# Attention: low products of two key tiles in the two halves of the array, values stored by head, fetches spread, and the order ranked by a table

## The chip, the cores and the metric

The kernel runs on one core of a Trainium2 chip. Its time is the device time of one execution in microseconds (us); the span is the time from the first to the last instruction of the profiled execution. The core has five engines, each with an instruction queue of its own that it works through in order: PE (TensorE, products and transposes by identity), DVE (VectorE), ACT (ScalarE), POOL (GpSimd) and SP (SyncE, which here issues DMAs). PE's weight loads are a row of their own, PEld, and run beside its products. Data lies in SBUF in 128 partitions, and PE writes into 8 banks of PSUM of 128 partitions x 512 f32 each.

## The reference

A two-layer decoder trunk over 2048 tokens of width 1024: a Mamba-2 layer, then multi-head latent attention with 16 heads, whose keys and values come from the stream after the first layer. The change lies in the causal attention:

```python
for i in range(S // Q_BLOCK):
    ...
    s = jnp.einsum('bqhd,bkhd->bhqk', q_nope[:, q0:kv_len], k_nope[:, :kv_len]) + \
        jnp.einsum('bqhr,bkr->bhqk', q_rope[:, q0:kv_len], k_rope[:, :kv_len])
    s = s.astype(jnp.float32) * scale
    p = jax.nn.softmax(jnp.where(mask, s, -jnp.inf), axis=-1).astype(v.dtype)
    outs.append(jnp.einsum('bhqk,bkhd->bqhd', p, v[:, :kv_len]))
```

The head's key has 64 + 32 (rotated) channels, its value 64. Everything is f32 in the reference.

## The kernel before

**Pairs of f16.** To keep f32 accuracy with fast products, a number is split into a high and a low f16 half. A score is three products (`mm3`, lines L291, L292, L293: high x high, high x low, low x high). A head's values lie in SBUF as 128 keys x 128 columns, 64 high and 64 low, so that one product of a probability tile with all 128 columns gives both; the two halves of the result's rows are added at the end.

**Stages.** Until about 2057 us the Mamba layer, the projections and the latent keys and values run; their results go to DRAM (`kn_d`, `kr_d` for keys without and with rotation, `qn_d`, `q1_d`, `q2_d` for queries, `v_d` for values). From 2057 to 2823 us attention runs, then the output projection (`back`), whose first steps a scheduler places among the last ones of attention. All but attention is ordered by that scheduler.

**Attention** is 64 jobs n: 16 heads x 4 query blocks of 512 (qb 0 to 3), each with 4·qb + 4 key tiles k of 128. A group c is four key tiles (512 keys), and j counts the four query tiles of a block. Tiles on the diagonal are narrower: 512, 384, 256 and 128 queries. A job's tasks have letters, and the profile shows them by these lines:

- S (L291 to L293, and L1453 for the mask): the scores of query tile j and group c into a bank, on PE. M (L1466) the row maximum and N (L1471, L1472) the shift, on DVE; E (L1477) the exponential into an f32 tile `Pr`, on ACT.
- Then a tile of probabilities has to be turned (keys on the partitions). Two ways: for the groups in TURNED (c = 0 in qb 1, c = 0 and 1 in qb 2 and 3), L (L1482, L1483, POOL) splits it into high and low f16 in `HL`, and X (L1487) turns it by a transposing DMA from SP's queue into `PX`, eight tiles of 128 x 512, four high and four low. For the others, T (L1491) turns it on PE into a bank, A (L1496, ACT) copies the high half and B (L1500, DVE) the low half into `PTs`.
- V (L1511, L1512): two products for each key tile, with the high and with the low probabilities, summed in one bank. F (L1516, ACT) and C (L1520, DVE) add the bank's two halves, and O (L1538) stores them.
- D (L1388, L1389, L1395, L1401 to L1403): fetches of the next head's K, V and Q on SP's queue. At the first score of each qb the Q of that block is fetched (three DMAs), and at qb 2 also K (two DMAs) and V (one), ahead of it.

**What sets the order.** `Pace` plays the tasks through with fixed durations and waiting times and writes down in which order they start; that is the order of every engine in the program. It tries eight plans of what PE prefers, and takes the shortest by its own account. Value products go in a fixed order: the tiles turned on PE first, those turned by DMA last. Buffers: 16 `Pr`, 5 `PTs`, 6 `HL`, 3 `PX`, 8 banks.

In the middle of the kernel, `L1099` (Mamba) and `L975` write products of 64 rows into a bank:

```python
for t in (slice(0, 64), slice(64, P)):
    nc.tensor.matmul(yi[t, hc], E[:, h, t], Xd[:, hc], start=True, stop=True)   # L1099
...
nc.tensor.matmul(ps[0:2 * H, :], w[:, k].rearrange("p n h -> p (n h)"), xT[k][:, n, :],   # L975, H = 32
...
nc.tensor.transpose(ps[:, c * 2 * H:(c + 1) * 2 * H], rt[:, c * P:(c + 1) * P],  # L982
                    self.ident[0:2 * H, 0:2 * H])
```

Of the kernel before, what the change touches and what calls it, by code (L numbers as in the profile page):

```python
# [22 lines left out]
P = 128  # L23
# [5 lines left out]
NH = 16  # L29
# [12 lines left out]
ENGINES = ("PE", "ACT", "DVE", "POOL", "SP")  # L42
# [3 lines left out]
TURNED = ((), (0,), (0, 1), (0, 1))  # L46

# [23 lines left out]
class Pace:  # L71

    def __init__(self, turned, prefer, scored, reserve):

        self.turned, self.now, self.count = turned, 0.0, 0
        self.prefer, self.most, self.reserve = prefer, scored, reserve
        self.jobs = [(h, qb) for h in range(NH) for qb in range(NB)]
        self.todo_s, self.todo_t, self.todo_v = [], [], []
        for n, (h, qb) in enumerate(self.jobs):
            self.todo_s += [(n, j, c) for j in range(4) for c in range(qb + 1)]  # L80
            tiles = [(n, k) for k in range(4 * qb + 4)]
            here = [t for t in tiles if t[1] // 4 not in turned[qb]]
            self.todo_t += here
            self.todo_v += here + [t for t in tiles if t not in here]
        for todo in (self.todo_s, self.todo_t, self.todo_v):
            todo.reverse()
        self.spare = {k: deque(range(n)) for k, n in BUFS.items()}
        self.slot = {}
        self.scored, self.sums = 0, []
        self.until = {e: 0.0 for e in ENGINES}  # L90
        self.ready = {e: [] for e in ENGINES if e != "PE"}
        self.coming, self.order = [], []
        self.maxima, self.probs, self.pairs, self.opened, self.dma = {}, {}, {}, {}, {}

# [7 lines left out]
    def at(self, t, f):  # L102
        self.count += 1
        heapq.heappush(self.coming, (t, self.count, f))

    def issue(self, e, what, busy, delay=0.0, after=None):
        self.order.append(what)
        self.until[e] = self.now + busy
        self.at(self.until[e], lambda: None)
        if after:  # L110
            self.at(self.until[e] + delay, after)

    def queue(self, e, rank, start, fits=lambda: True):
        self.count += 1
        self.ready[e].append((rank, self.count, fits, start))
# [7 lines left out]
    def run(self):  # L123
        while True:
            for e, waiting in self.ready.items():
                if self.until[e] <= self.now:
                    fit = sorted((w for w in waiting if w[2]()), key=lambda w: w[:2])
                    if fit:
                        waiting.remove(fit[0])
                        fit[0][3]()  # L130
            if self.until["PE"] <= self.now:
                self.tensor()
            if not self.coming:
                break
            self.now = self.coming[0][0]
            while self.coming and self.coming[0][0] <= self.now:
                heapq.heappop(self.coming)[2]()
        assert not (self.todo_s or self.todo_t or self.todo_v)
        return self.order

    def tensor(self):
        banks = len(self.spare["ps"])
        if self.sums and banks:
            return self.rows(self.sums.pop())
        for kind in self.prefer:
            if kind == "S" and self.todo_s and banks > self.reserve and self.scored < self.most:
                return self.scores(*self.todo_s.pop())
            if kind == "T" and self.todo_t and banks and self.spare["PTs"]:
                n, k = self.todo_t[-1]
                if all((n, j, k // 4) in self.probs for j in range(self.first(n, k), 4)):  # L150
                    return self.turn(*self.todo_t.pop())
            if kind == "V" and self.todo_v and self.todo_v[-1] in self.pairs:
                if banks or self.todo_v[-1][0] in self.opened:
                    return self.values(*self.todo_v.pop())

    def scores(self, n, j, c):
# [3 lines left out]
        if j == c == 0:  # L160
            self.queue("SP", 2, lambda: self.issue("SP", ("D", n), 3500 if qb == 2 else 1800))

        def maximum():
            self.issue("DVE", ("M", n, j, c), 65 + w * 1.042, 116, counted)

        def counted():
            self.maxima[n, j] = self.maxima.get((n, j), 0) + 1
            if self.maxima[n, j] == qb + 1:
                self.queue("DVE", 1, lambda: self.issue("DVE", ("N", n, j), 250 if qb else 70, 120, shift))

        def shift():
            for x in range(qb + 1):
                self.queue("ACT", 2, lambda x=x: self.exp(n, j, x), lambda: self.spare["Pr"])

        self.issue("PE", ("S", n, j, c), 3 * (w / 2.4 + 2.5) + 60 * (c == qb), 200,
                   lambda: self.queue("DVE", 2, maximum))

    def exp(self, n, j, c):
        w = self.width(n, j, c)
        self.take("Pr", n, j, c)  # L180

        def freed():
            self.give("ps", "S", n, j, c)
            self.scored -= 1

        def done():
            if (j, c) == (3, NB - 1):
                self.queue("DVE", 3, lambda: self.issue("DVE", ("R", n), 450, 2000, summed))
            if c in self.turned[self.jobs[n][1]]:
                self.queue("POOL", 1, lambda: self.split(n, j, c),  # L190
                           lambda: self.spare["HL"] and ((n, c) in self.dma or self.spare["PX"]))
            else:
                self.probs[n, j, c] = w // P

        def summed():
            self.sums.append(n)

        self.issue("ACT", ("E", n, j, c), 245 + w * 0.832, 175, freed)
        self.at(self.until["ACT"] + 330, done)

    def split(self, n, j, c):
# [5 lines left out]
        def moved():  # L207
            self.give("Pr", n, j, c)
            self.queue("SP", 1, lambda: self.issue("SP", ("X", n, j, c), 1550, DMA_DELAY, landed))

        def landed():
            self.give("HL", n, j, c)
            self.dma[n, c] -= 1
            if not self.dma[n, c]:
                for k in range(4 * c, 4 * c + 4):
                    self.pairs[n, k] = "PX"
# [3 lines left out]
    def rows(self, n):  # L220
        self.take("ps", "Y", n)
        self.issue("PE", ("Y", n), 110, 200, lambda: self.queue("ACT", 2, lambda: self.issue(
            "ACT", ("Z", n), 160, 200, lambda: self.give("ps", "Y", n))))

    def turn(self, n, k):
        jj = self.first(n, k)
        w = (4 - jj) * P
        self.take("ps", "T", n, k)
        self.take("PTs", n, k)

        def done():
# [4 lines left out]
            self.queue("ACT", 1, lambda: self.issue("ACT", ("A", n, k), 55 + w * 0.835, 150,  # L236
                                                    lambda: self.queue("DVE", 1, low)))

        def low():
            self.issue("DVE", ("B", n, k), 65 + w * 1.042, 260, split)  # L240

        def split():
            self.give("ps", "T", n, k)
            self.pairs[n, k] = "PTs"
# [3 lines left out]
    def values(self, n, k):  # L248
        w, qb = (4 - self.first(n, k)) * P, self.jobs[n][1]
        if n not in self.opened:  # L250
            self.opened[n] = 4 * qb + 4
            self.take("ps", "O", n)
        self.opened[n] -= 1
        last = not self.opened[n]

        def done():
            if self.pairs[n, k] == "PTs":
                self.give("PTs", n, k)
            else:
                c = k // 4  # L260
                self.dma[n, c] -= 1
                if self.dma[n, c] == -4:
                    self.give("PX", n, c)
            if last:
                self.queue("ACT", 0, lambda: self.issue("ACT", ("F", n), 620, 60, lambda: self.queue(
                    "DVE", 0, lambda: self.issue("DVE", ("C", n), 598, 260, closed))))

        def closed():
            self.give("ps", "O", n)
            self.queue("SP", 0, lambda: self.issue("SP", ("O", n), 600))  # L270

        self.issue("PE", ("V", n, k), 2 * (w / 2.4 + 2.5), 200, done)


class Net:
# [987 lines left out]
    def mla_kv_down(self, b, tables):  # L1263
# [13 lines left out]
        self.rope(pk[0], pk[1], *tables, self.kr_d[0:16], self.kr_d[16:32], 16, b * TB,  # L1277
# [31 lines left out]
    def mla_up(self, b, tables):  # L1309
# [31 lines left out]
        while ahead:  # L1341
            (n, w), ahead = ahead, next(todo, None)
            qT = self.qT
            for i in range(2 if n == 6 else 4):
# [4 lines left out]
                elif n < 4:  # L1349
# [7 lines left out]
                    c0 = (n - 2) * 1024  # L1357
# [385 lines left out]
```

## Time and profile before

| | us |
|---|---|
| median of 3 runs (3016.37 to 3019.53) | 3016.63 |
| profiled execution, its own time | 3009.45 |
| its span | 3007.7 |
| PE busy in the span | 2892.3 (96%) |
| DVE busy | 2160.8 (72%) |
| ACT busy | 1813.6 (60%) |
| POOL busy | 977.0 (32%) |
| attention, first score to last value product | 2057 to 2823 |

A row of a group or timeline reads: line, engine, operation, written tile <- read tiles, shape (for PE "rows*columns" of the weights used, then the moving data), count; busy time and mean ns; and behind a bar or in brackets the idle time before it with what ended it. A product's busy time covers its drain too, which lies under the next one; so in a stream the distance of the starts is its price. "mm" and "tr" are the two names of the banks. SPq rows are the instructions of SP's queue, which issue DMAs.

### The profile page before, as it was taken

Reading aid. Unit: us, or ns where it says so; the run is one execution under the profiler, and the core shown is the slowest. Engines: PE = TensorE matmul, PEld = TensorE weight load, DVE = VectorE, ACT = ScalarE, POOL = GpSimd, SP = SyncE. Lnnn points to the kernel's source line nnn. Section 1 sums busy time; section 2 is a strip of 40 time slices with the busy share of each in tenths; the row PEclk is TensorE's granted clock in tenths of the full one; section 3 lists DMA queues with packets and bytes.
Section 4 is the critical chain, followed back from the end, with each engine's and each line's share of the span. In section 5 each row is a group of like instructions: output and inputs, shape, how many; then the busy total and the mean of one; then the engine's idle time right before and its main releaser. Section 6 shows DMA issues by size and latency. Waiting matters only on the chain.

```text
span 3007.7 us, 48921 instructions
## 1 busy us (share of the span) xinstructions
PE 2892.3 (96%) x16535; PEld 1793.7 (60%) x16535; DVE 2160.8 (72%) x4539; ACT 1813.6 (60%) x4632; POOL 977.0 (32%) x1206
## 2 busy tenths in 40 slices
PE   8999999999999999999999999999999999998998
PEld 6777745555565555655566545544555555554687
DVE  6878887778777777878665564456887888877476
ACT  7888586566755546556553443335777777776422
POOL 1212021112121221212111121225777777777300
PEclk9999999999999999999999999999999999999999
DMA  5353657655565335554445655656899899999784
GB/s 184 102 162 96 212 179 264 192 163 171 192 222 180 125 113 188 191 190 168 140 140 205 233 176 175 201 178 154 170 169 176 166 175 172 171 182 193 178 273 160
DMA packets 586415, 532.21 MB, mean 177 GB/s; under 512 B 396770, under 2 KB 450274, under 8 KB 584724
## 3 DMA queue, kind: packets, MB, share of 16 engines
q1 hardware_dynamic: 574180, 490.94, 60.3%
q0 software_dynamic: 11984, 38.15, 3.4%
q8 instruction: 130, 2.13, 0.3%
q14 instruction: 121, 0.99, 0.1%
HBM read 332.21 MB, written 112.86 MB: 148 GB/s over the span
## 4 chain that ended last, share of the span: by engine, by line
PE 57%; DVE 14%; DMA 10%; ACT 9%; issue 5%; POOL 4%; SPq 1%; ACTq 0%; DVEq 0%; POOLq 0%
PE mm L291 11%; PE mm L293 11%; PE mm L292 11%; PE tr L291 4%; PE tr L293 4%; PE tr L292 4%; DVE cacc L895 3%; DMA PX<-HL 3%; DMA big<-cumT 1%; DMA wraw<-in_ssm_w_in_dram 1%; PE mm L1511 1%; ACT Xw L1092 1%; PE tr L1099 1%; PE mm L1512 1%; POOL HL L1482 1%
## 5 line engine op out<-in xcount | busy, mean ns | idle before, releaser
L1483 POOL TENSOR_TENSOR HL<-Pr,HL 128x512 f16<-128x512 f32 x320 | 369.8, 1156 | 25.5
L291 PE MATMUL mm<-xT,wsp 128*128 128x512 f16 (+1 forms) x800 | 308.7, 386 | 0.4 <-ACT wsp L329 0.4
L292 PE MATMUL mm<-xT,wsp 128*128 128x512 f16 (+1 forms) x800 | 306.0, 382 | 0.0
L293 PE MATMUL mm<-xT,wsp 128*128 128x512 f16 (+1 forms) x800 | 304.6, 383 | 0.4 <-DVE wsp L322 0.2
L1048 POOL TENSOR_TENSOR Xp<-Xw,Xp 128x512 fp32r<-128x512 f32 x64 | 86.5, 1351 | 610.4 <-ACT Xp L1047 597.9
L1482 POOL CAST HL<-Pr 128x512 f16<-128x512 f32 x320 | 195.7, 612 | 157.7 <-ACT Pr L1477 105.4
L1477 ACT ACTIVATE Pr<-mm,nm 128x512 f32<-128x512 f32 (+3 forms) x322 | 201.0, 629 | 71.0 <-DVE nm L1472 66.3
L1477 ACT ACTIVATE Pr<-tr,nm 128x512 f32<-128x512 f32 (+3 forms) x318 | 197.5, 626 | 66.4 <-DVE nm L1472 63.2
L291 PE MATMUL mm<-wsp,xT 128*128 128x512 f16 (+2 forms) x640 | 233.8, 367 | 3.5 <-ACT craw L889 2.2
L895 DVE SCALAR_TENSOR_TENSOR cacc<-craw,pack,cacc 128x512 f32<-128x512 f32 x288 | 217.3, 774 | 26.0 <-ACT cacc L893 24.2
L292 PE MATMUL mm<-wsp,xT 128*128 128x512 f16 (+2 forms) x640 | 233.3, 365 | 1.4 <-DVE wsp L330 1.3
L293 PE MATMUL mm<-wsp,xT 128*128 128x512 f16 (+2 forms) x640 | 232.8, 364 | 0.0
L1466 DVE TENSOR_REDUCE mx<-tr 128x1 f32<-128x512 f32 (+3 forms) x318 | 186.4, 604 | 45.5 <-PE tr L1453 30.9
L1466 DVE TENSOR_REDUCE mx<-mm 128x1 f32<-128x512 f32 (+3 forms) x322 | 190.8, 605 | 29.4 <-PE mm L293 14.9
L291 PE MATMUL mm<-wsp,yT 128*128 128x512 f32 x512 | 210.0, 411 | 1.5 <-DVE sz L925 1.1
L292 PE MATMUL mm<-wsp,yT 128*128 128x512 f32 x512 | 204.0, 399 | 0.0
L293 PE MATMUL mm<-wsp,yT 128*128 128x512 f32 x512 | 203.3, 398 | 0.0
L293 PEld LDWEIGHTS <-xT 128*128 128x128 f16 (+1 forms) x1280 | 125.0, 98 | 118.8 <-issue 4.9
L1076 ACT ACTIVATE big<-big,d_cum 128x128 f32<-128x128 f32 x512 | 168.1, 391 | 43.4 <-DMA big<-cumT 43.3
L292 PEld LDWEIGHTS <-xT 128*128 128x128 f16 (+1 forms) x1280 | 126.0, 98 | 114.4 <-issue 14.5
L291 PEld LDWEIGHTS <-xT 128*128 128x128 f16 (+1 forms) x1280 | 125.6, 98 | 115.1 <-issue 6.8
L1092 ACT ACTIVATE Xw<-tr,d_wend 128x64 f32<-128x64 f32 x512 | 111.7, 328 | 129.4 <-DVE y L1089 102.8
(469 smaller groups left out, 7735.8 us busy)
## 6 DMA issues: line engine op xcount, KB each, us to landing
wsp<-wo_d SPq DMA_DIRECT2D x96, 512.0 KB, 3.8
wsp<-w_d SPq DMA_DIRECT2D x68, 512.0 KB, 4.2
wraw<-in_ssm_w_in_dram SPq DMA_DIRECT2D x128, 256.0 KB, 3.2
big<-cumT SPq DMA_DIRECT2D x64, 512.0 KB, 4.9
wo_d<-wsp SPq DMA_DIRECT2D x32, 512.0 KB, 3.5
w_d<-wsp SPq DMA_DIRECT2D x32, 512.0 KB, 3.5
st<-w_d SPq DMA_DIRECT2D x56, 256.0 KB, 2.9
wsp<-wu_d SPq DMA_DIRECT2D x28, 512.0 KB, 3.7
```

The costliest lines, as they stand in the source:

```text
L291: mm(out, l_hi, r_hi, start=start, stop=False)
L292: mm(out, l_hi, r_lo, start=False, stop=False)
L293: mm(out, l_lo, r_hi, start=False, stop=stop)
L895: nc.vector.scalar_tensor_tensor(acc, raw[:, k:k + TB], wk[k], acc, ALU.mult, ALU.add)
L1048: nc.gpsimd.tensor_tensor(u[:, 1], x, u[:, 0].bitcast(F32), ALU.subtract)
L1076: act(E[:, h, :], E[:, h, :], AF.Relu, bias=ncum[:, h0 + h:h0 + h + 1])
L1092: act(Xw[:, hc], px[:, hc], AF.Copy, scale=wend[:, h0 + h:h0 + h + 1])
L1099: nc.tensor.matmul(yi[t, hc], E[:, h, t], Xd[:, hc], start=True, stop=True)
L1466: v.tensor_reduce(m[:, at:at + 1], s, AX.X, ALU.max, negate=True)
L1477: nc.scalar.activation(tile("Pr", n, j, c)[:, :w], bank("S", n, j, c)[:, :w], AF.Exp, bias=moves[(4 * n + j) % len(moves)], accum_out=sums ...
L1482: nc.gpsimd.tensor_copy(u[:, 0], x)
L1483: nc.gpsimd.tensor_tensor(u[:, 1], x, u[:, 0], ALU.subtract)
```

## The change

The high and low product of a key tile are separated. For the tiles in LOWS (4 tiles in qb 1, all 12 in qb 2, all 16 in qb 3), V does the high product only; when a block's tiles have had theirs, a new task W multiplies the low probabilities with the high values alone, 64 columns wide: even tiles into partitions 0 to 63 of the bank, odd ones into 64 to 127, in turn. (The product of low values and low probabilities is left out there.) High and low tiles have buffers of their own for this, `PH` (5) and `PL` (14, eight of them in the unused half of a key buffer, four in a former activation tile).

Values are stored by head (`v_d` is 16 x 128 x 16 x 128), so that a head's are read in one piece of 4 KB per partition. Rotated queries and keys are stored with both halves of the rotation side by side, and the rotated keys, which are the same for all heads, stay in both key buffers instead of being fetched for every head. The next head's Q comes in two fetches of two DMAs (at qb 0 and 2), K in two halves (qb 1 and 2), V at qb 3. Q, K and V have fixed places by head.

The order is no longer the best of eight plans. Each task has a rank from a table (by letter and place in the head) plus its head's number, and each engine starts the ready task of the lowest rank. Value products may go in any order within a block, and two blocks may be open at once.

```diff
-BUFS = dict(ps=8, Pr=16, PTs=5, HL=6, PX=3)
-PLANS = [(p, s, r) for p in ("TSV", "STV") for s in (5, 6) for r in (0, 1)]
+BUFS = dict(ps=8, Pr=16, PH=5, PL=14, HL=6, PX=3)
+MOST = 6
+DRAIN = 212
+LOWS = ((), ((0, 1, 2, 3),), (tuple(range(12)),), (tuple(range(16)),))
+RANKS = {
+    "S": "7735 344 732 4486 -631 9611 -3703 222 -978 281 305 -101 4274 -1728 204 3590 -1046 173 8785 "
...
+    def key(self, task):
+        kind, n, *at = task
+        h, qb = self.jobs[n]
...
+        return h + self.rank[kind][i] - 100 * (kind in "CFZ")
...
+    def do_V(self, n, k):
...
+        both = not self.paired(n, k)
...
+        self.issue("PE", ("V", n, k), (1 + both) * (w / 2.4 + 2.5), 200, done)
+
+    def do_W(self, n, g):
+        group = LOWS[self.jobs[n][1]][g]
...
+        self.issue("PE", ("W", n, g), DRAIN + sum((4 - self.first(n, k)) * P / 2.4 + 6 for k in group[::2]), 200, done)
...
-                    c0 = (n - 2) * 1024
-                    nc.gpsimd.dma_start(self.v_d[t0 + i * P:t0 + (i + 1) * P, c0:c0 + 1024], u)
+                    h0 = 8 * (n - 2)
+                    nc.gpsimd.dma_start(self.v_d[h0:h0 + 8, :, 4 * b + i].rearrange("h p d -> p h d"),
+                                        u.rearrange("p (h d) -> p h d", h=8))
...
+    def load_kr(self, lo, hi):
+        ts = slice(lo * TB, hi * TB)
+        for K in self.K:
+            self.nc.gpsimd.dma_start(K[64:96, 0:2, ts], self.kr_d[:, :, :, ts].rearrange("r q s t -> (r q) s t"))
...
         def D(n):
             h, qb = jobs[n]
             if h + 1 < NH:
-                if qb == 2:
-                    self.load_k(h + 1, 0, NB, nc.sync)
+                if qb in (0, 2):
+                    self.load_q(h + 1, qb, nc.sync)
+                if qb in (1, 2):
+                    self.load_k(h + 1, 2 * qb - 2, 2 * qb, nc.sync)
+                if qb == 3:
                     self.load_v(h + 1, nc.sync)
-                self.load_q(h + 1, qb, nc.sync)
...
+        def product(n, k, rows, weights, low):
+            o = bank("O", n)[rows, pace.first(n, k) * P:]
...
+            nc.tensor.matmul(o, weights, half(n, k, low), start=start, stop=not left[n][at[0]])
 
         def V(n, k):
...
-            nc.tensor.matmul(o, vals[h][:, k, :], hi, start=left == 4 * qb + 3, stop=False)
-            nc.tensor.matmul(o, vals[h][:, k, :], lo, start=False, stop=left == 0)
+            both = not pace.paired(n, k)
+            w = vals[jobs[n][0]][:, k, :]
+            product(n, k, slice(0, P), w, 0)
+            if both:
+                product(n, k, slice(0, P), w, 1)
+
+        def W(n, g):
+            for i, k in enumerate(LOWS[jobs[n][1]][g]):
+                half_rows = slice(64 * (i % 2), 64 * (i % 2) + 64)
+                product(n, k, half_rows, vals[jobs[n][0]][:, k, 0:64], 1)
```

Two places in the order show it. First, PE at the diagonal tiles of the last query block of the 10th head. Before, every key tile has its product with the high tile (L1511) and the low tile (L1512) behind each other, with weights of 128 columns; T's transposes (L1491) stand between. The names behind the arrow are the probabilities (`PTs`) and the values (`xT`, the pool that V and Q use):

```order
L1512 MATMUL mm_21089<-PTs_21122,xT_25513 128x384
L1511 LDWEIGHTS xT_25513
L1511 MATMUL mm_21089<-PTs_21123,xT_25513 128x256
L1512 LDWEIGHTS xT_25513
L1512 MATMUL mm_21089<-PTs_21123,xT_25513 128x256
L1491 MATMUL mm_21088<-pack,Pr_21109 128x128
L1491 MATMUL mm_21088<-pack,Pr_21101 128x128
```

Now the low products stand together at the end of the block, 64 rows high; `K` and the second `xT` are places of `PL`, and the row of L401 is the next job's score:

```order
L1650 MATMUL mm_21079<-PL_21122,xT_20881 64x512
L1650 LDWEIGHTS xT_20881
L1650 MATMUL mm_21079<-K_20008,xT_20881 64x384
...
L1650 MATMUL mm_21079<-xT_21121,xT_20881 64x256
...
L1650 MATMUL mm_21079<-xT_21121,xT_20881 64x128
L401 LDWEIGHTS xT_20878
L401 MATMUL tr_21085<-K_20007,xT_20878 128x256
```

The low products of the block moved from their places beside the high ones into one closing group.

Second, SP's queue where the fetches for the 11th head stand. Before, twelve of them follow each other, those of qb 1, 2 and 3, between two transposing DMAs:

```order
L1487 DMA_TRANSPOSE PX_21117<-HL_21114 128x8x128
L1401 DMA xT_26014<-qn_d 64x2x512
L1402 DMA xT_26014<-q_d 16x2x512
L1403 DMA xT_26014<-q_d 16x2x512
L1388 DMA K_26036<-kn_d 64x4096
L1389 DMA K_26036<-kr_d 32x4096
L1395 DMA xT_26039<-v_d 128x16x128
L1401 DMA xT_26041<-qn_d 64x2x512
L1402 DMA xT_26041<-q_d 16x2x512
L1403 DMA xT_26041<-q_d 16x2x512
L1401 DMA xT_26079<-qn_d 64x2x512
L1402 DMA xT_26079<-q_d 16x2x512
```

After it, at qb 2 and 3 of a head:

```order
L1524 DMA xT_20878<-qn_d 64x2x1024
L1525 DMA xT_20878<-qr_d 32x2x1024
L1501 DMA K_20007<-kn_d 64x2x1024
L1686 DMA o_d<-Os_25851 64x512
L1619 DMA_TRANSPOSE PX_21109<-HL_21104 128x8x128
L1619 DMA_TRANSPOSE PX_21109<-HL_21105 128x8x128
L1619 DMA_TRANSPOSE PX_21109<-HL_21106 128x8x128
L1686 DMA o_d<-Os_25921 64x512
L1619 DMA_TRANSPOSE PX_21110<-HL_21107 128x8x128
L1619 DMA_TRANSPOSE PX_21111<-HL_21108 128x8x128
L1619 DMA_TRANSPOSE PX_21111<-HL_21103 128x8x128
L1518 DMA xT_21117<-v_d 128x2048
```

The fetches moved apart: three and one, with output stores and transposing DMAs between them.

More of the change, by code (lines that the diff above doesn't have):

```diff
@@ L110, in issue @@
         if after:
[L111 to L115, printed above, removed]
+            self.at(self.until[e] + delay, after, *task[1:])
     def take(self, k, *owner):
@@ L124, in run @@
         while True:
[L125 removed]
+            for e in ENGINES[1:]:
                 if self.until[e] <= self.now:
[L127 to L130, printed above, removed]
+                    self.start(e, [t for t in self.ready[e] if self.fits(t)])
             if self.until["PE"] <= self.now:
@@ L136, in run @@
             while self.coming and self.coming[0][0] <= self.now:
-                heapq.heappop(self.coming)[2]()
-        assert not (self.todo_s or self.todo_t or self.todo_v)
+                _, _, f, args = heapq.heappop(self.coming)
+                f(*args)
+        assert not self.todo and not any(self.ready.values()) and not any(self.opened.values())
         return self.order
-    def tensor(self):
[L142 to L154, printed above, removed]
@@ L160, in scores @@
         if j == c == 0:
[L161 to L173, printed above, removed]
@@ new lines, in probable @@
+    def probable(self, n, j, c):
+        qb = self.jobs[n][1]
+        if (j, c) == (3, NB - 1):
+            self.ready["DVE"].append(("R", n))
+        if c in TURNED[qb]:
+            self.ready["POOL"].append(("L", n, j, c))
+            return
+        self.probs[n, j, c] = self.width(n, j, c) // P
+        for k in range(4 * c, 4 * c + 4):
+            if (n, k) not in self.turned and all((n, i, c) in self.probs for i in range(self.first(n, k), 4)):
+                self.turned.add((n, k))
+                self.ready["PE"].append(("T", n, k))
@@ L235, in done @@
                     self.give("Pr", n, j, k // 4)
[L236 to L244, printed above, removed]
-        self.issue("PE", ("T", n, k), (4 - jj) * 109, 200, done)
-    def values(self, n, k):
+            self.ready["ACT"].append(("A", n, k))
@@ L249, in values @@
+    def do_V(self, n, k):
         w, qb = (4 - self.first(n, k)) * P, self.jobs[n][1]
         if n not in self.opened:
-            self.opened[n] = 4 * qb + 4
+            self.opened[n] = 4 * qb + 4 + len(LOWS[qb])
             self.take("ps", "O", n)
-        self.opened[n] -= 1
[L254 to L272, printed above, removed]
+        both = not self.paired(n, k)
+        self.summed.add((n, k))
+        for g, group in enumerate(LOWS[qb]):
+            if k in group and all((n, x) in self.summed for x in group):
+                self.ready["PE"].append(("W", n, g))
+        def done(n, k):
+            if self.pairs[n, k] == "PE":
+                self.give("PH", n, k)
+            if both:
+                self.low_read(n, k)
+            self.count_down(n)
```

325 lines of the change are left out of this document (225 added, 100 removed).

## The prediction

> **What bounds the kernel now.** I first read where attention stands in the span and which engine is full there: a table of busy time by stretch, for the whole attention stage (first score near 2057 us, last value product near 2823 us), its middle and its end. The columns are us of busy time of PE, weight loads, DVE, ACT and POOL (records in brackets), granted clock, DMA share, GB/s.
>
> ```profile
> 2057.00:2823.00 766.00, 727.13 (x4369) 416.73 (x4368) 609.79 (x1518) 577.40 (x1690) 574.82 (x665) 0.98 0.91 171
> 2100.00:2730.00 630.00, 611.04 (x3736) 353.50 (x3735) 517.00 (x1290) 488.62 (x1443) 474.82 (x560) 1.00 0.94 173
> 2730.00:2823.00 93.00, 77.42 (x418) 42.77 (x417) 59.03 (x134) 58.91 (x156) 69.20 (x68) 0.91 0.77 159
> ```
>
> The stage is TensorE's: 97% busy in the middle, DVE 82%, ACT and POOL under 80%. The DMA engines at 0.94 are the next limit. What a product costs in a stream is read from the starts on PE's timeline, since its busy time includes the drain under the next product:
>
> ```profile
> 2499.95 0.38 PE L1512 MATMUL mm<-PX,xT 128*128 128x512 f16 x1
> 2500.17 0.27 PE L291 MATMUL tr<-K,xT 96*128 96x256 f16 x1
> 2500.28 0.27 PE L292 MATMUL tr<-K,xT 96*128 96x256 f16 x1
> ...
> 2500.50 0.22 PE L1453 MATMUL tr<-mk,idb 128*128 128x128 bf16 x1
> 2500.56 0.28 PE L1491 MATMUL tr<-pack,Pr 128*128 128x128 f32 x1
> 2500.67 0.38 PE L1511 MATMUL mm<-PX,xT 128*128 128x512 f16 x1
> 2500.89 0.38 PE L1512 MATMUL mm<-PX,xT 128*128 128x512 f16 x1
> 2501.10 0.38 PE L291 MATMUL mm<-K,xT 96*128 96x512 f16 x1
> ```
>
> So 512 columns take 0.216 us, 256 take 0.110, 128 take 0.056, and a turned f32 tile 0.110; 384 lies between, 0.163. With the loops' counts (per head 84 scores and 56 value products of 512 columns, 12 and 8 each of 384, 256 and 128, 16 masks, 56 turned tiles) that is 43.9 us a head, 702 us for 16. The stage lasts 766, so 64 us are lost, the half-speed clock after long waits included. The waits of PE name the largest part, and PE's and SyncE's timelines at one of them (the 10th head) show its cause:
>
> ```profile
> PE mm L1511 <- DMA PX<-HL: 12.0, 8, 2.4
> PE tr L1511 <- DMA PX<-HL: 6.4, 6, 1.8
> ```
>
> ```profile
> 2553.05 0.38 PE L293 MATMUL mm<-K,xT 96*128 96x512 f16 x1
> 2555.86 0.38 PE L1511 MATMUL mm<-PX,xT 128*128 128x512 f16 x1 [2.42 <-DMA PX<-HL]
> ```
>
> ```profile
> 2524.09 6.65 SPq L1487 DMA_TRANSPOSE PX<-HL  x4
> 2530.79 0.59 SPq L1401 DMA_DIRECT2D xT<-qn_d  x1
> ...
> 2533.98 0.41 SPq L1395 DMA_DIRECT2D xT<-v_d  x1
> 2534.50 3.72 SPq L1401 DMA_DIRECT2D xT<-qn_d  x1
> ...
> 2540.83 0.59 SPq L1403 DMA_DIRECT2D xT<-q_d  x1
> 2541.53 4.02 SPq L1487 DMA_TRANSPOSE PX<-HL  x3
> ```
>
> Twelve fetches for the next head stand in one row on SyncE, one of them held 3.72 us, and for 10.7 us no transposing DMA is issued. The transposes behind land late, and PE waits. Such waits come about once a head: 14 of them, 18.4 us.
>
> **Part 1: the low products.** Of the 40 key tiles of a head, 32 get their low product in the closing step W: 12 pairs of 512 columns, two of 512 beside 384, two of 256 beside 128. If two run at once, a pair lasts as long as its wider one plus a step between starts. No row shows this for f16 and 512 columns. The nearest rows are in the Mamba stage, where L1099 already writes the two halves of a bank in turn, against L982, with f32 products of 64 columns on one place, and L975, f16 and 512 columns wide, always on the same half:
>
> ```profile
> 85.75 0.40 PE L293 MATMUL mm<-xT,wsp 128*128 128x512 f32 x1
> 86.08 1.15 PE L1099 MATMUL tr<-Xd,big 128*64 128x64 f32 x32
> 87.16 0.50 PE L291 MATMUL mm<-xT,wsp 128*128 128x512 f32 x1
> ```
>
> ```profile
> 361.08 0.46 PE L982 MATMUL tr<-pack,yt 64*128 64x64 f32 x4
> 355.97 0.47 PE L293 MATMUL mm<-wsp,yT 128*128 128x512 f32 x1
> 356.38 3.64 PE L975 MATMUL tr<-xT,wraw 128*64 128x512 f16 x16
> 359.95 0.50 PE L291 MATMUL mm<-wsp,yT 128*128 128x512 f32 x1
> ```
>
> ```profile
> L1099 PE MATMUL tr<-Xd,big x2048: 222/222/369, 86.1 to 1569.0; 128*64 128x64 f32 x187
> L982 PE MATMUL tr<-pack,yt x16: 221/222/272, 25.6 to 1134.9; 64*128 64x64 f32 x16
> L975 PEld LDWEIGHTS <-wraw x48: 106/110/110, 356.4 to 1132.7; 128*64 128x64 f16 x48
> ```
>
> Taking off the last record's 0.222: L1099 starts 32 passes in 0.93 us, 0.030 apart; L982 starts 4 in 0.24, 0.08 apart. L975, on one half, keeps 0.216 for 512 columns. So halves do run side by side. I take a step of 0.007, and a pair of 512 as 0.223 instead of 0.432: 12 x 0.209 + 2 x 0.156 + 2 x 0.050 = 2.92 us a head, 46.7 us. Bounds: 0 if they don't overlap, and 48 without the step.
>
> Going into halves and out costs too. Before L1099, 0.33 us pass from a product of 0.216: 0.11 extra; behind its last start, at 87.01, 0.15 pass instead of 0.03 to 0.06: 0.1. So 0.2 a visit; L975 gives 0.41 - 0.216 in and about 0.1 out, 0.3. There are 3 visits a head, 48 in all: 10 to 14 us. I take 10, as in L1099's rows the halves alternate as in W. Net: -37 us, all on PE.
>
> Here a rule speaks against the change. The Trainium skill, "TensorE: Matmul & The Clock Gate", Part 3, says that a weight load overlaps running products only when its row group differs; in W every load has all 128 rows. By that rule each pair would pay two loads, and the gain would be gone. The trace disagrees: L975's loads of 0.110 us have all rows as well and are hidden, 16 products in 3.64 us. The Trainium skill's same part also states 2.38 times for three column tiles; an estimate from it for two, 0.243 a pair, would leave 5 us less of the gain.
>
> **Part 2: fetches.** The fetches of a head fall from 15 issues (12 for Q, 2 for K, 1 for V) to 7, at most three in a row, and Q, K and V have places of their own by head, so that SyncE doesn't meet the wait of 3.72. Eight issues of 0.59 less are 4.7 us a head off SyncE, which hides behind nothing that matters except those transposes. I take away the 18.4 us of waits above. Bounds: none of it, or 30, when half of the other 46 us lost goes too.
>
> **Part 3: the order.** All five engines' rows are ranked anew. Counting what stands in PE's rows between the last score of a group of turned tiles and the first value product on it, priced as above, I get a median of 22.8 us before and 13.1 now (least 12.3 and 10.3). What has to happen in between: reduction, shift, exponentials, then on POOL and through a transposing DMA
>
> ```profile
> L1483 POOL TENSOR_TENSOR HL<-Pr,HL 128x512 f16<-128x512 f32 x320 | 369.8, 1156 | 25.5
> L1482 POOL CAST HL<-Pr 128x512 f16<-128x512 f32 x320 | 195.7, 612 | 157.7 <-ACT Pr L1477 105.4 <-DMA PX<-HL 31.5 <-ACT PTs L1496 16.2
> DMA to landing us min/median/max: 3.1/3.3/5.5
> ```
>
> two POOL turns of 1.77 for the last rows of two groups, 3.3 for the landing and some 3 for DVE and ACT: about 10. It fits, with 3 us to spare where there were 13. I charge 4 us of new waits, a fifth of the old ones; bounds 0 and, at 1.5 us for each of 48 groups, 72. PX also stays held until W; that is in these bounds.
>
> **Part 4: the rest.** V is stored in pieces of 256 bytes instead of rows of 2 KB, 32 stores on POOL's queue ahead of attention, and read in 4 KB rows. An issue with 2048 such pieces took POOL 1.18 us:
>
> ```profile
> L1358 POOL DMA_DIRECT2D v_d<-big x12: 539/539/586, 1634.4 to 2016.0; - x12
> L1395 POOL DMA_DIRECT2D xT<-v_d x1: 1180/1180/1180, 2008.0 to 2008.0; - x1
> DMA packets 392559, 130.62 MB, mean 171 GB/s; under 512 B 373696, under 2 KB 385088, under 8 KB 391040
> ```
>
> With half as many pieces a store takes POOL some 0.3 us more and lands perhaps 2 us later (an estimate, from the step between the two rows). PE is covered there by the gate products, and I charge 1 us, between 0 and 6 (eight stores of each of four blocks, 0.2 each). In attention the 15 reads of V leave 2048 small packets each, of the 373,696 that the stage's DMA view counts, and rotated K is not read again: DMA work falls by about 8%, PE's by 5%, so its share stays near 0.9 and it doesn't become the bound. PL adds buffers, not copies; POOL, DVE and ACT do the same work as before.
>
> **Sum.** -46.7 + 10 - 18.4 + 4 + 1 = -50 us on a span of 3007.7; the profiled execution took 3009.45, and the median of the runs is 3016.63, 9 us above the span. 2957.6 and 9 give 2966 us.
>
> **The rivals.**
> - Only the products gain. SyncE's relief is eaten by other waits, as the landing was only the last of several: -36 to -20, 2981 to 2997. For it speaks that 46 of the 64 us lost aren't transposes, and the end of the stage, where ACT stood behind a weight:
>
> ```profile
> 2763.73 1.06 ACT L1565 ACTIVATE W<-wr 128x1024 fp32r<-128x1024 f32 x1 [4.91 <-DMA wr<-in_mla_w_out_dram]
> 2765.51 0.69 PE L1491 MATMUL tr<-pack,Pr 128*128 128x128 f32 x2 [4.86 <-ACT Pr L1477]
> ```
>
>   These rows of the later projection still stand among ACT's last attention rows.
> - The order gains more: the end's loss is halved as well, 25 to 30 us more, 2938.
> - The other side: the 3 us to spare are too few. Place: the first product on PX of each of the 48 groups. Today's waits are 1.3 us each; at 1.5 for all, 72 us instead of 4, 3034. It decides the sign from 1.1 us a group on. Against it: landings keep to 3.1 to 5.5.
> - Halves don't overlap: the 46.7 are missing, 3013, no change.
> - Loads aren't hidden: 256 pairs at two loads of 0.11, +56 us on the forecast, 3022. The Trainium skill's rule named above describes this case.
>
> **How the numbers follow.** The forecast (2950 to 2978) gets 0.52, products alone 0.21, more from the order 0.12, late transposes 0.08, no overlap 0.04, loads 0.03. A measurement here can't tell 0.2%, 6 us, from no change. Faster: the first three and a little, 0.86; the same: no overlap and 0.01 of the loads and late cases, 0.05; slower: 0.09. For 8 in 10 the range holds the forecast, products alone and the nearer half of what the order may add: 2935 to 3000.
>
> **What would show it.** The stage should last some 716 us instead of 766. W's timeline should show 16 products of 64 columns wide halves in about 1.9 us and a gap of 0.1 at each side; single low products should remain 8 a head. SyncE should have no row of fetches over 2 us, and PE's waits for PX should fall under 8 us. Wrong would be: W's starts 0.216 apart, loads that end a wait on W, or PX waits over 50 us.

## The result, and the profile after

The changed kernel takes 2949.74 us (median of 4 runs, 2948.85 to 2951.47) beside 3017.59 for the kernel before: ratio 0.9775, 95% interval 0.9758 to 0.9792, 68 us less. Run once more with the experiments below it gave 2950.69, ratio 0.9776 (0.9763 to 0.979). The forecast was 2966 with a range of 2935 to 3000, so the result lies inside the range, at the lower edge of the 2950 to 2978 that the main forecast stood for. The profiled execution took 2951.47 us, its span is 2949.7, 58 less than the span before.

The table of busy time by stretch, in the columns used before: first the whole attention stage, first score to last value product, then its steady middle.

```profile
2056.90:2761.80 704.90, 684.33 (x4386) 396.00 (x4384) 603.84 (x1518) 582.00 (x1688) 570.97 (x664) 0.99 0.94 178
2200.00:2600.00 400.00, 395.70 (x2560) 229.02 (x2558) 353.42 (x887) 339.28 (x991) 327.05 (x389) 1.00 0.99 182
```

The same middle before:

```profile
2200.00:2600.00 400.00, 387.23 (x2360) 223.45 (x2358) 326.40 (x812) 307.60 (x909) 299.35 (x355) 1.00 0.94 172
```

The stage lasts 704.9 us instead of 766.6, 62 less; it starts 1 us later, and what follows it takes 3 us more. In the middle PE is 99% busy (97% before), and the DMA engines are now 99% busy as well.

W on PE's timeline, the closing step of a last query block (sixteen products, whose pairs start together; the first row holds two products of 128 columns and the first eight of the visit) and of a third one (its first row is the last product of 128 columns). One passage through W is called a visit from here on:

```profile
2405.60 1.58 PE L1650 MATMUL mm<-PX,xT 128*128 128x512 f16 x10
2407.02 0.38 PE L1650 MATMUL mm<-xT,xT 128*64 128x512 f16 x1
2407.02 0.38 PE L1650 MATMUL mm<-K,xT 128*64 128x512 f16 x1
...
2407.87 0.28 PE L401 MATMUL tr<-K,xT 96*128 96x256 f16 x1
...
2429.30 0.38 PE L1650 MATMUL tr<-PH,xT 128*128 128x512 f16 x1
2429.60 1.05 PE L1650 MATMUL tr<-PX,xT 128*64 128x512 f16 x8
```

Two products of 512 columns start within 0.003 to 0.004 us of each other, and the next pair 0.216 later (0.240 behind the first pair of a visit). From the first start of a visit to PE's next instruction pass 0.555 us for 4 products, 1.307 for 12 and 1.740 for 16 (medians over 16 heads). A visit starts some 0.31 us behind a product of 512 columns that costs 0.216 in a stream (2429.30 to 2429.60 above), so entering costs 0.09.

SyncE's queue over most of a head, from a second profile of the changed kernel (to be held against the twelve fetches in a row), and PE's waits for transposes in the first one:

```profile
2297.17 0.59 SPq L1524 DMA_DIRECT2D xT<-qn_d  x1
2297.80 0.59 SPq L1525 DMA_DIRECT2D xT<-qr_d  x1
2298.50 3.27 SPq L1619 DMA_TRANSPOSE PX<-HL  x2
...
2314.74 0.58 SPq L1524 DMA_DIRECT2D xT<-qn_d  x1
2315.37 0.60 SPq L1525 DMA_DIRECT2D xT<-qr_d  x1
2316.01 0.59 SPq L1501 DMA_DIRECT2D K<-kn_d  x1
2316.71 0.55 SPq L1686 DMA_DIRECT2D o_d<-Os  x1
2317.35 4.33 SPq L1619 DMA_TRANSPOSE PX<-HL  x3
...
2327.28 0.57 SPq L1518 DMA_DIRECT2D xT<-v_d  x1
2327.95 6.09 SPq L1619 DMA_TRANSPOSE PX<-HL  x4
```

```profile
PE tr L1650 <- DMA PX<-HL: 4.9, 5, 1.3
PE mm L1650 <- DMA PX<-HL: 1.9, 2, 1.5
```

Before, thirteen heads each had a row of twelve fetches that lasted 10.4 to 11.6 us; now at most three follow each other, for 1.9 us at most (one of 2.7 in the first profile), and PE's waits for PX went from 18.4 us (14 times) to 6.8 (7). The burst, as the row of twelve is called below, had a second mark that the forecast did not read. A row of POOL's waits before, and below it, of the changed kernel, the list of all that waited for the transposing DMA (us, times):

```profile
POOL HL L1482 <- DMA PX<-HL: 31.5, 17, 5.3
```

```profile
  PEld L1650: 5.5, 7
  PE tr L1650: 4.9, 5
  PE mm L1650: 1.9, 2
```

Before, about once a head POOL waited for an `HL` buffer that a late transpose had not emptied; now it is not in the list.

### The profile page after: what moved, and what is told of

The parts are those of the page before. It is cut to its first block, busy times and chain, and to the rows that moved or that the text cites. A ratio compares the mean times of both kernels' runs of the same rounds, so it can differ in the third digit from the quotient of the medians.

```text
span 2949.7 us, 48867 instructions
## 1 busy us (share of the span) xinstructions
PE 2851.2 (97%) x16535; PEld 1772.5 (60%) x16535; DVE 2155.0 (73%) x4539; ACT 1820.5 (62%) x4632; POOL 986.9 (33%) x1200
## 4 chain that ended last, share of the span: by engine, by line
PE 53%; DVE 13%; issue 11%; ACT 8%; DMA 8%; POOL 6%; SPq 1%; POOLq 0%; ACTq 0%; DVEq 0%
PE mm L401 10%; PE mm L402 10%; PE mm L403 10%; PE tr L1650 4%; DVE cacc L1005 3%; PE tr L401 3%; PE tr L402 3%; PE tr L403 3%; DMA wraw<-in_ssm_w_in_dram 2%; POOL HL L1615 2%; DMA big<-cumT 2%; PE mm L1623 1%; PE tr L1209 1%; DMA PX<-HL 1%; ACT big L1186 1%
## 5 line engine op out<-in xcount | busy, mean ns | idle before, releaser
L401 PE MATMUL mm<-xT,wsp 128*128 128x512 f16 (+1 forms) x800 | 308.3, 385 | 0.2 <-ACT wsp L439 0.2
L1609 ACT ACTIVATE Pr<-mm,nm 128x512 f32<-128x512 f32 (+3 forms) x356 | 221.1, 625 | 65.5 <-DVE nm L1604 51.7
L401 PE MATMUL mm<-wsp,xT 128*128 128x512 f16 (+2 forms) x640 | 234.0, 367 | 3.2 <-ACT craw L999 2.0
L1598 DVE TENSOR_REDUCE mx<-mm 128x1 f32<-128x512 f32 (+3 forms) x356 | 211.7, 608 | 31.6 <-PE mm L403 19.4
L401 PE MATMUL mm<-wsp,yT 128*128 128x512 f32 x512 | 210.1, 411 | 1.5 <-DVE sz L1035 1.1
L401 PEld LDWEIGHTS <-xT 128*128 128x128 f16 (+1 forms) x1280 | 125.4, 98 | 107.6 <-issue 17.8
L1598 DVE TENSOR_REDUCE mx<-tr 128x1 f32<-128x512 f32 (+3 forms) x284 | 166.0, 597 | 20.2 <-PE tr L1583 16.5
L1609 ACT ACTIVATE Pr<-tr,nm 128x512 f32<-128x512 f32 (+3 forms) x284 | 174.1, 618 | 10.7 <-DVE nm L1604 8.8
```

The source lines that it names most:

```text
L401: mm(out, l_hi, r_hi, start=start, stop=False)
L1598: v.tensor_reduce(m[:, at:at + 1], s, AX.X, ALU.max, negate=True)
L1609: nc.scalar.activation(tile("Pr", n, j, c)[:, :w], bank("S", n, j, c)[:, :w], AF.Exp, bias=moves[(4 * n + j) % len(moves)], accum_out=sums ...
```

## The experiments

The experiments ran in three sets, each beside the kernel before. The columns: the ratio to the kernel before in the same set; the stage in the profile; the time from one head's first score to the next head's on PE's timeline (second to thirteenth head); PE's gaps, the time between starts beyond the earlier product's own width, summed where over 0.1 us; PE's waits for PX, as the rows of the transposing DMA list them; and the DMA share from 2200 to 2600 us.

| kernel | ratio (95%) | stage | a head | gaps | PX waits | DMA |
|---|---|---|---|---|---|---|
| before | 1 | 766.6 | 44.7 to 47.3 | 55.8 | 18.4 | 0.94 |
| changed, first profile | 0.9775 (0.9758-0.9792) | 704.9 | 41.9 to 43.2 | 31.3 | 6.8 | 0.99 |
| changed, again | 0.9776 (0.9763-0.979) | 702.7 | 41.9 to 42.4 | 28.2 | 3.5 | 0.98 |
| lows in one half | 0.9893 (0.9878-0.9909) | 731.6 | 44.5 to 44.9 | 15.8 | 3.7 | 0.92 |
| lows in two blocks | 0.9831 (0.9815-0.9847) | 712.7 | 42.8 to 43.8 | 24.3 | 4.0 | 0.97 |
| lows beside the highs | 0.9997 (0.9987-1.0006) | 766.3 | 46.6 to 46.9 | 59.4 | 2.1 | 0.87 |
| old fetches | 1.0101 (1.0088-1.0115) | 802.4 | 48.7 to 51.3 | 125.5 | 77.1 | 0.82 |
| one burst | 1.0007 (0.9996-1.0018) | 773.9 | 44.7 to 49.5 | 97.1 | 50.9 | 0.85 |
| small pieces, spread | 0.9941 (0.9923-0.9959) | 751.2 | 43.3 to 50.0 | 76.8 | 36.9 | 0.90 |
| old order, new fetches | 0.9881 (0.9868-0.9895) | 738.7 | 44.72 | 28.2 | 0 | 0.94 |
| the same, visits of four | 0.9867 (0.985-0.9883) | 727.1 | 43.2 to 45.7 | 33.2 | 0.5 | 0.94 |

**All low products in one half.** The edit in W (the stop counts follow it):

```diff
-                half_rows = slice(64 * (i % 2), 64 * (i % 2) + 64)
+                half_rows = slice(64, P) if i == len(group) - 1 else slice(0, 64)
```

> The changed kernel (2950 us), with the low products of a visit all in the lower 64 columns one after another, and only a visit's last product in the upper 64; order, storage and fetches stay. My theory (the gain of the products is that two run at once): a head's three visits then hold 3 + 11 + 14.25 widths of 512 in a row where the pairs take 2 + 6 + 7.5, so 12.75 x 0.213 = 2.7 us more a head, 43 us in all: 2993 us, and a visit of 12 products takes about 2.4 us instead of 1.31. Rival (the gain lies in taking the low products out of the stream and into a block of their own, or in the new order, and TensorE would have had the time anyway): below 2960 us.

The visits took 0.767, 2.332 and 3.198 us, 2.70 more a head, as expected, and a head 44.53 instead of 41.88. Over 16 heads that is 43 us. The ratio rose by 0.0117, 35 us, and the stage by 29 (from 702.7): PE's gaps shrank from 28.2 to 15.8 us and took 12 back. On its profile, a visit of twelve:

```profile
2402.51 1.91 PE L1651 MATMUL tr<-PX,xT 128*64 128x512 f16 x8
2404.05 0.86 PE L1651 MATMUL tr<-K,xT 128*64 128x128 f16 x4
2404.84 1.53 PE L1623 MATMUL mm<-pack,Pr 128*128 128x128 f32 x12
```

It lasts from 2402.51 to 2404.84. So running two at once is worth 2.65 us in a head of the even middle of the stage, and 29 to 35 us in all; the rival fell.

**Lower half first, then upper.**

```diff
-                half_rows = slice(64 * (i % 2), 64 * (i % 2) + 64)
+                half_rows = slice(0, 64) if 2 * i < len(group) else slice(64, P)
```

> The changed kernel, with the same low products in the same two halves of the columns, but the first half of a visit's tiles all in the lower columns and then the second half all in the upper, instead of turn by turn. If a product can start ahead of those before it only while a single one waits (the trace showed one 128-wide product start 0.05 us ahead of the 256-wide one in front of it), the two runs overlap in one product: 41 us more, 2990 us, and the visit of 12 takes about 2.4 us. Rival (each half has a queue of its own, some products deep): no change, 2950 us, and 1.31 us a visit; something between says how deep.

Neither end: the visits took 0.558, 1.554 and 2.420 us. A visit of sixteen, in the program eight products on `PX` for the lower half and then eight on `xT`, `K` and `PL` for the upper (the first row holds two products of 128 columns and the first five of the lower half):

```profile
2410.68 1.79 PE L1650 MATMUL mm<-PX,xT 128*128 128x512 f16 x7
2412.10 0.40 PE L1650 MATMUL mm<-xT,xT 128*64 128x512 f16 x1
2412.31 0.38 PE L1650 MATMUL mm<-PX,xT 128*64 128x512 f16 x1
2412.34 0.38 PE L1650 MATMUL mm<-K,xT 128*64 128x512 f16 x1
2412.52 0.38 PE L1650 MATMUL mm<-PX,xT 128*64 128x512 f16 x1
2412.55 0.38 PE L1650 MATMUL mm<-PL,xT 128*64 128x512 f16 x1
2412.74 0.38 PE L1650 MATMUL mm<-PX,xT 128*64 128x512 f16 x1
```

The ninth product of the program starts at 2412.10, ahead of the sixth, seventh and eighth (2412.31, 2412.52, 2412.74). In the visits of twelve the seventh starts with the third, again past three that wait. So a product overtakes up to three that wait for the other half. The upper run thus begins four products late in a visit of sixteen and two in one of twelve, and makes up a part of it since its last tiles are narrower. Per head that is 0.93 us more in the visits, and a head took 0.91 more.

**Low products back beside the high ones, in the changed order.**

```diff
-            both = not pace.paired(n, k)
+            both = True
...
         def W(n, g):
...
+            pass
```

> The changed kernel in its own order, with every low product as 128 columns right behind its high product, as before the change, and nothing at the place of the visits; storage, fetches and the order of all else stay. My theory: the 38 us of TensorE work come back and the order keeps the rest of its gain: 2988 us (2980 to 2995), with lost time in the stage as after (about 40 us). Rival (the order holds only with the short visits, since its slack was made for them): 3000 us or more. Against the run with all in one half, the difference is what 48 visits cost to enter and leave: that run should be 5 to 10 us slower than this one.

The rival held: 0.9997, the whole gain gone, though only 38 us of PE work came back. The run with all in one half, which I had put 5 to 10 us above this one, was 32 us below it. PE's waits:

```profile
PE mm L401 <- ACT Pr L1609: 16.0, 21, 3.8
PE tr L401 <- DVE Os L1667: 6.4, 15, 0.7
PE tr L401 <- ACT Pr L1609: 6.0, 15, 0.5
```

Four scores and a value product wait for a bank at the same five places of nearly every head, 2.5 us a head. The order's rows are timed for short value products, and with long ones it is worse than the old order with the same products and fetches (0.9881). Which instruction is late there stays open.

**The fetches as before, in the changed order.** D again issues three loads at qb 0 and twelve more at qb 2, all in one row (the text below says eleven, and leaves V and the last two query tiles out of it; in the edit and the trace they are part of it):

```diff
-                if qb in (0, 2):
-                    self.load_q(h + 1, qb, nc.sync)
...
+                if qb == 2:
+                    self.load_q1(h + 1, 1)
+                    self.load_k(h + 1, 0, NB, nc.sync)
+                    nc.sync.dma_start(self.K[(h + 1) % 2][64:96, 0:2], self.kr_d.rearrange("r q s t -> (r q) s t"))
...
```

`load_q1` is three loads, one of `qn_d` and two of `qr_d`.

> The changed kernel in its own order, but SyncE fetches a head's operands as before: three loads in its first query block, in the third a burst of eleven more that holds four loads of K, and the rotated keys of each head anew (the fourth block's value load and the last two query tiles with six loads as after). My theory (the waits for PX that came once a head went with the burst): they come back, 12 to 18 us: 2956 to 2962 us where the changed kernel takes 2944. Rival (the new order puts the transposes' readers later, and the waits would have gone with the old fetches too): under 4 us more, and no fixed PX wait in each head.

99 us more, some six times what I expected, and 1% slower than the kernel before. PE's and POOL's waits:

```profile
PE tr L1664 <- DMA PX<-HL: 75.7, 15, 6.6
```

```profile
POOL HL L1628 <- DMA PX<-HL: 49.1, 17, 4.5
```

One wait of 5.0 us in each head, and the granted clock of the stage fell to 0.93 (0.99 in the changed kernel). PE's timeline shows where:

```profile
2323.49 0.58 PE L1664 MATMUL tr<-PX,xT 128*128 128x512 f16 x1 [5.47 <-DMA PX<-HL]
2323.87 0.63 PE L401 MATMUL mm<-K,xT 96*128 96x512 f16 x1
2324.30 0.63 PE L402 MATMUL mm<-K,xT 96*128 96x512 f16 x1
```

Behind the wait the products of 512 columns stand 0.427 us apart instead of 0.216 until 2329.4, at a granted clock of 0.50. Of the 125.5 us of gaps, 80 are the waits for PX measured from start to start, and 35 lie between 171 products that follow at such a distance (5.5 in the changed kernel). A wait thus cost PE almost half as much again.

**The new fetches in the old order**, with the old planner and both products in 128 columns:

```diff
-LOWS = ((), ((0, 1, 2, 3),), (tuple(range(12)),), (tuple(range(16)),))
+LOWS = ((), (), (), ())
+PLANS = [(p, s, r) for p in ("TSV", "STV") for s in (5, 6) for r in (0, 1)]
```

> The order of before (its planner) with both products of a tile in 128 columns, but the new fetches (spread over the blocks), the new layout of V and the rotated keys loaded once. My theory: the once-a-head PX waits go, 14 of 18 us, as the fetches alone cause them: 0.995 of the kernel before (2997 us where that takes 3011). Rival (spreading the fetches does nothing for an order that wasn't made for it): 1.000 within 0.2%.

More than I expected: 0.9881, 35 us. In the stage PE has the same products, by kind and shape, in the same order as before, so that storage, places and fetches are what differs. A head took 44.72 us, every time; before, that was the best head, and the others took up to 2.6 more. Its profile names no instruction that waited for PX, and the gaps went from 55.8 to 28.2 us. So this part is worth 28 us of the stage, in the old order.

**Burst or pieces?** The two halves of the old fetches apart, in the changed order. One burst of the large loads, and the small pieces spread:

```diff
-                if qb in (0, 2):
-                    self.load_q(h + 1, qb, nc.sync)
...
+                if qb == 2:
+                    self.load_q(h + 1, 0, nc.sync)
+                    self.load_k(h + 1, 0, 2, nc.sync)
+                    self.load_q(h + 1, 2, nc.sync)
+                    self.load_k(h + 1, 2, 4, nc.sync)
+                    self.load_v(h + 1, nc.sync)
```

> The changed kernel in its own order and with its own large loads (seven a head: two of Q's parts for each half, two of K, one of V), but all seven issued together in a head's third query block, as one burst on SyncE. The old pieces in the old places had cost 99 us (3049.5 against 2950.7), and this tells whether the burst or the pieces did it. Theory A (the burst: SyncE's queue holds the transposes behind it, and the first load waits for its buffer): 1.00 of the kernel before or more, with one PX wait of several us a head. Theory B (the number of pieces and of small packets, 96 rows cut in five instead of two): under 0.98, no fixed wait.

```diff
+                if qb in (0, 2):
+                    self.load_q1(h + 1, qb)
+                    self.load_q1(h + 1, qb + 1)
+                if qb == 1:
+                    nc.sync.dma_start(self.K[(h + 1) % 2][64:96, 0:2], self.kr_d.rearrange("r q s t -> (r q) s t"))
...
```

> The changed kernel in its own order, with the old small pieces (12 loads of Q a head instead of 4, and the rotated keys loaded anew for each head), but spread over the four query blocks like its own loads. Theory A (the burst): under 0.985 of the kernel before, that is at most 20 us over the changed kernel, since SyncE's nine more issues of 0.6 us have room beside 42 us of a head. Theory B (the pieces): 1.00 or more, as with the old fetches whole.

For the burst theory A held: 1.0007, with a wait for PX in nearly every head. But the pieces cost too, and lie between both theories at 0.9941. Against the changed kernel's 0.9776 the burst costs 0.023 (70 us) and the pieces 0.0165 (50 us), the two together 99. What waited for the transposing DMA, with the burst and (below) with the pieces:

```profile
  PE tr L1650: 49.4, 14
  POOL HL L1614: 29.7, 16
```

```profile
  PE tr L1664: 25.2, 24
  PE mm L1664: 11.7, 9
```

So the POOL wait is the mark of a burst: one stop a head, 1.9 us on average here and in the kernel before, 2.9 with the old fetches whole; PE's own stop is 3.5 us here. The pieces make many small ones of PE (33 of some 1.1 us) and none of POOL. SyncE's own rows suggest why these find little room (argued, not tried): a head has 20 transposes at 1.28 us (median of 320), four stores and a sum's store at about 0.5, and seven loads at 0.59, some 32 of 41.9 us; nine loads more make it 38.

**The old planner with low products side by side**, in groups of four (eight visits a head):

```diff
+            elif k % 4 == 3:
+                W(n, k // 4)
...
+            for i, k in enumerate(range(4 * c, 4 * c + 4)):
```

> The old planner with the new fetches (the run that took 0.988 of the kernel before), and now low products side by side there too, of the same tiles as in the changed kernel, but by groups of four right behind the fourth high product: eight visits a head instead of three. A group of four of 512 columns takes 0.555 us and 0.09 us to enter where four in a row take 0.864: 0.22 us less, six of them a head; the two groups with narrower tiles gain nothing: 1.3 us a head, 21 us. My theory (the products bring what they are worth in the old order too, and the search brings only fewer visits): 0.981 (2961 us where the kernel before takes 3017). Rival (only the searched order turns the products' time into a shorter stage): 0.985 or more.

The visits took 0.555 us, as expected, and the stage became 11.6 us shorter where I had expected 21; 5 us of the rest are more gaps. The runs moved by 0.0014 only, inside their intervals. So the rival is nearer: in the old order half of the gain expected arrives in the stage, and little in the runs. Of the 24 us between this stage and the changed kernel's, five visits fewer a head make some 17 (0.555 + 0.09 - 0.432 = 0.21 each, 80 of them), and the gaps 5. What the ranked order is worth beyond longer visits is therefore not separated: the old planner with three visits a head was not tried.

**The end of the stage.** Three kernels try to win back its last 100 us, where PE still loses some 20 us in gaps, and where VectorE and ScalarE wait for loads of the output projection. Of the changed kernel's waits from 2640 to 2770 us:

```profile
DVE xT L1732 <- DMA xT<-ri_d: 5.7, 1, 5.7
ACT W L1713 <- DMA wr<-in_mla_w_out_dram: 5.4, 3, 3.3
PE mm L401 <- ACT Pr L1609: 9.0, 5, 4.5
```

```diff
-                early = b == 0 and k < 2
+                early = b == 0 and k < 1
```

> The changed kernel, with the gating of only one of the two early row blocks of the part behind attention drawn into attention's last 100 us; the other one follows with the rest behind it. My theory: VectorE's wait of 5.68 us at 2709 us (for a load that SyncE issues behind three transposes) goes with it, and so most of TensorE's wait of 4.53 us behind it: 2945 us. Rival: the second block is then late in the part behind attention and costs there what it gave: 2950 us, or more, with a wait of some us behind the last value product.

```diff
-            if h == NH - 3:
+            if h == NH - 4:
```

> The changed kernel, with the first four loads of the output weights one head earlier (behind head 12's blocks instead of head 13's). ScalarE waited three times for such loads in attention's last 110 us (1.30, 0.86 and 3.28 us), and TensorE behind it 3.8 us at 2689 us. My theory: the first two waits go and the third one's load leaves earlier too, so 3 to 5 us less than the changed kernel: 2940 us where that takes 2944. Rival (the third load waits for its buffer and not for its turn, and the tail is set by the other waits): no change.

> Both late edits at once: the output weights' first loads one head earlier, and the gating of only one early row block. Alone, the first gave a stage of 699.6 us and the second one of 694.9 where the changed kernel has 702.7 to 704.9, the second with 4 us more behind it. If they add up: a stage of 691 us and 2938 us (0.975). Rival (both shorten the same stall): as the better one alone, 2942 us or more.

The first gave a stage of 694.9 us, 10 less than the changed kernel's first profile, but 4 more behind it: 0.9781 (0.9765 to 0.9798). Its theory held for the stage, as PE's wait of 4.5 us at 2716 is gone, and its rival behind it, where PE's first wait for `oT` grew from 4.3 to 7.4 us. The second 699.6 and 0.977 (0.9755 to 0.9785). Both together 701.0 and 0.9789 (0.9768 to 0.9809): they do not add up. Of the waits with both, in the same part:

```profile
PE mm L401 <- ACT Pr L1609: 8.1, 2, 4.5
```

PE's wait of 4.5 us there is back, at 2695 us, and behind the stage the one of 7.4 stayed. None of the three can be told from the changed kernel, and no version here beats it.

## Why the prediction was right, and where it was not

**Part 1, the low products, was right in mechanism and size.** With the prices from PE's rows, PE's work fell by 38 us; -37 was forecast. The step between two starts was 0.003 instead of 0.007, and entering and leaving a visit costs 0.09 and 0.1, the 0.2 taken (with 0.024 more behind the first pair). The rivals without overlap and with visible loads fell: the loads of 64 columns and 128 rows stay hidden in W (pairs 0.216 apart), so the trace disagrees with the rule of the Trainium skill, "TensorE: Matmul & The Clock Gate", Part 3, that a weight load overlaps only where its row group differs. What the forecast left out is that these 38 us are not the price of taking the step back: in the changed order that costs 67 us (lows beside the highs), and in the old order, in visits of four, the products brought 4 us by the runs and 18 by the profiled spans.

**Part 2, the fetches, was too small: -18.4 against -28 in the stage.** The step that failed is "I take away the 18.4 us of waits above": it takes a wait for PX at its idle time alone. Between before and the old order with the new fetches, 27.6 us of gaps went. Of these 20.7 are the same waits measured from start to start, some 5 lie between products that follow a wait at half the clock (0.43 us apart from 2327.4 to 2329.4, at a granted clock of 0.50), and 2 are the balance of other waits. The forecast had named that slow stretch among the 64 us lost, but gave it no price in this sum. The other end that I had given, 30, was nearer, by luck: half of the other 46 us on top of 18.4 would be 41. The burst also stopped POOL once a head (31.5 us); whether that cost PE anything of its own is not shown.

**Part 3, new waits from the tighter order: +4 forecast, 0 to 3 found.** Gaps are 28.2 and 31.3 us in the two profiles of the changed kernel, 28.2 in the old order with the new fetches. The new waits for PX themselves are 3.5 and 6.8 us, where that run has none, so +4 was right for them; the other gaps are some 5 us smaller. The rival of late transposes didn't come with the new fetches; with the old ones it came in full (75.7 us in 15 waits of 5.0, where I had put 1.1 us for each of 48 groups as the point that decides; 48 is the number of blocks that use PX, which hold 80 groups). So the 3 us to spare were enough only with SyncE's queue cleared, and the two parts are no sum: the new fetches bring 35 us in the old order and 99 in the new one.

**Part 4.** The start of the stage shows no cost of V's small stores (+0.9 and -2.3 us; +1 forecast). Behind the stage 2.7 and 3.8 us came that I didn't have. PE's first wait there is some 3 us longer, before and after (4.2 in the second profile):

```profile
PE mm L291 <- ACT oT L321: 1.4, 1, 1.4
```

```profile
PE mm L401 <- ACT oT L431: 4.3, 1, 4.3
```

Why ACT delivers `oT` later there was not tried. My account of the DMA engines was wrong: I had their work fall by 8% and the share stay near 0.9. Share times head gives 43.3 us before (0.94 x 46.05, the mean head) and 41.2 to 41.9 after (0.98 x 42.04, 0.99 x 42.36), 3 to 5% less, while a head became 8 to 9% shorter.

**The sum.** In spans -50 was forecast, and -58.0 and -62.4 came. The 9 us that I added from the profiled execution to the median don't belong to the change: they are the spread of the kernel before, whose runs reached from 3004.76 to 3022.24 us over the sets, with heads of uneven length. Both misses point the same way, and make up the 16 us between 2966 and 2950. The first is the fetches'; that the second, the spread, is theirs too is only likely, as the old order with the new fetches has even heads.

## What to carry to other kernels

Before adding to a queue whose transfers another engine waits for, add up that queue's own time per round and look for every engine that waits for it, not only for the one that is the bound: here a burst showed as one stop a round on the producer's buffers. Price a long wait of PE with the slow products behind it, and not at its idle time alone. An order that is searched for one set of durations was no gain by itself: with longer products its stage was 28 us longer than the old planner's, and with the old fetches the kernel took 99 us more than with its own. When a stage gets shorter, set each resource's work per round beside the new length: here the DMA engines' 41 us stand beside a head of 42, so further savings on PE alone should bring little (argued, not tried).

## What the runs showed of the hardware

Two products in different column halves run as independent streams: 0.003 us between their starts, pairs of 512 columns 0.216 apart as single products are, and a product may start ahead of up to three earlier ones that wait for the other half. The Trainium skill, "TensorE: Matmul & The Clock Gate", Part 3, has products start strictly in program order; these rows disagree (2412.10 ahead of 2412.31, 2412.52 and 2412.74), at least across halves. In every longer run (6 and 8 products for one half ahead of the other, and 11 and 15 in the kernel with all but one in one half) the first product of the other half starts with the one that has three of its own half still behind it. So PE doesn't work through its queue strictly in order, and the program needs no strict alternation, but by these rows runs of five or more for one half leave the other idle.
